# Taking one DMA engine's share of two stores away: a batched A·Bᵀ kernel, where part of two stores moves to GpSimd's DMA queue

## Chip, cores and metric

The kernel runs on one core of one Trainium2 chip. The metric is device time in microseconds (us) of one execution, the median of several runs. Before the change it is 125.15 us (three runs, 124.94 to 125.19).

## What is computed

Sixteen independent products of 512×512 float32 matrices, the second one transposed:

```python
def setup_inputs():
    batch, m, k, n = 16, 512, 512, 512
    return {"a": np.random.randn(batch, m, k).astype(np.float32),
            "b": np.random.randn(batch, n, k).astype(np.float32)}

def reference(a, b):
    return np.matmul(a, b.transpose(0, 2, 1)).astype(np.float32)
```

The inputs are 2 × 16 MiB and the output is 16 MiB, so 50.3 MB have to cross between HBM and SBUF in any case.

## The kernel before

The batches are worked in eight pairs. A load brings `a` or `b` of a whole pair (2 MiB, 16 KiB to each of 128 partitions) into one of seven slots of `ld`. VectorE casts it to bf16, TensorE transposes it into PSUM (`tp`), ScalarE and VectorE bring the transposes back (`ta`, `tb`), TensorE multiplies into `ps`, and ScalarE copies the products into one of seven slots of `ob`. SyncE stores each batch from there (1 MiB, 8 KiB from each partition).

Loads are issued by ScalarE (the trace calls this queue q10), stores by SyncE (q1), and GpSimd has a third queue (q0). All three feed the same 16 DMA engines.

```python
NL = 7; NO = 7
X = 11
ld = sbuf("ld", [P, NL, 2 * J, K], f32)
ob = sbuf("ob", [P, NO, J, N], f32)            # J = 4 rows of 512 per partition and batch
turn = sbuf("turn", [P, 4, 2, 16], f32)        # a small load's target, read by nobody
...
def load(n, engine):
    u, slot = n // 2, n % NL
    src = (a if n % 2 == 0 else b)[2 * u:2 * u + 2].rearrange("e (p j) k -> (e p) j k", j=2 * J)
    engine.dma_start(ld[:, slot], src).then_inc(s_ld[slot], 16)

def landed(n):
    return s_st[n % NO], 16 * (n // NO + 1)

def store(n, lo=0, hi=J, step=1, part=slice(0, P), engine=nc.sync):
    rows = slice(lo, hi, step)
    return engine.dma_start(
        out[n].rearrange("(p j) n -> p j n", j=J)[part, rows], ob[part, n % NO, rows])
...
# GpSimd: tells VectorE which load has landed; then its part of batch 11's store
for n in range(2 * pairs):
    nc.gpsimd.wait_ge(s_ld[n % NL], 16 * (n // NL + 1)).then_inc(s_go, 1)
nc.gpsimd.wait_ge(s_out, X + 1)
for i in range(4):
    nc.gpsimd.dma_start(turn[:5, i], a[0, :5, :64]...[:, :, :16]).then_inc(s_y, 16)
    for part in (slice(20 + i, 32, 4), slice(96 + i, P, 4)):
        store(X, step=J - 1, part=part, engine=nc.gpsimd).then_inc(s_y, 16)

# SyncE: no store before load 7 has landed
nc.sync.wait_ge(s_ld[0], 32)
for n in range(batch):
    nc.sync.wait_ge(s_out, n + 1)
    if n != X:
        store(n, hi=J if n < batch - 1 else J - 1).then_inc(landed(n)[0], 16)
        continue
    store(n, lo=1, hi=J - 1).then_inc(landed(n)[0], 16)
    store(n, step=J - 1, part=slice(32, 96)).then_inc(s_x, 16)
    for i in range(4):
        store(n, step=J - 1, part=slice(i, 16, 4)).then_inc(s_x, 16)
    store(n, step=J - 1, part=slice(16, 20)).then_inc(s_x, 16)
...
# ScalarE, per pair: its loads, then the products into ob
for e in range(2):
    n = 2 * u + e
    if n >= NO:
        nc.scalar.wait_ge(*landed(n - NO))     # the slot's earlier store has landed
    for j in range(J):
        ...                                     # copy ps -> ob[:, n % NO, j]
...
# end
nc.scalar.wait_ge(s_x, 16 * 6)
nc.scalar.wait_ge(s_y, 16 * 12)
for n in range(batch - NO, batch):
    nc.scalar.wait_ge(*landed(n))
```

[...] The four `turn` loads of five rows move nothing that is needed[...]. The other pieces of batch 11's rows 0 and 3 are cut so that engine 4[...] has less to move than the others.

Of the kernel before, what the change touches and what calls it, by code (L numbers as in the profile page):

```python
# [10 lines left out]
def kernel(  # L11
# [6 lines left out]
    nc = tc.nc  # L18
    P = 128
    batch, M, K = a.shape  # L20
    _, N, _ = b.shape
    J = M // P
# [4 lines left out]
    f32 = mybir.dt.float32  # L27
    bf16 = mybir.dt.bfloat16
    NL = 7
    NO = 7  # L30
    X = 11

    def sbuf(name, shape, dtype):
        return ctx.enter_context(nc.sbuf_tensor(name, shape, dtype))

    def sem(name):
        return tc.alloc_semaphore(name)

    with tc.tile_critical(no_gpsimd_drain=True):  # L41
# [6 lines left out]
        ta = sbuf("ta", [P, KO, 2 * J * P], bf16)  # L48
        tb = sbuf("tb", [P, KO, 2 * J * P], bf16)
        ob = sbuf("ob", [P, NO, J, N], f32)  # L50
        turn = sbuf("turn", [P, 4, 2, 16], f32)
        tp = ctx.enter_context(nc.psum_tensor("tp", [P, 4, 2 * J, P], bf16))
        ps = ctx.enter_context(nc.psum_tensor("ps", [P, 4, N], f32))

# [2 lines left out]
        s_st = [sem(f"s_st{i}") for i in range(NO)]  # L57
# [13 lines left out]
        s_out = sem("s_out")  # L71
        s_x = sem("s_x")
        s_y = sem("s_y")
# [5 lines left out]
            out=ident[:], in_=ident[:], compare_op=mybir.AluOpType.not_equal, fill=1.0,  # L79
# [6 lines left out]
        def load(n, engine):  # L86
            u, slot = n // 2, n % NL
            src = (a if n % 2 == 0 else b)[2 * u:2 * u + 2].rearrange(
                "e (p j) k -> (e p) j k", j=2 * J
            )  # L90
            engine.dma_start(ld[:, slot], src).then_inc(s_ld[slot], 16)

        def landed(n):
            return s_st[n % NO], 16 * (n // NO + 1)

        def store(n, lo=0, hi=J, step=1, part=slice(0, P), engine=nc.sync):
            rows = slice(lo, hi, step)
            return engine.dma_start(  # L98
                out[n].rearrange("(p j) n -> p j n", j=J)[part, rows], ob[part, n % NO, rows]
            )  # L100

        load(0, nc.scalar)
# [3 lines left out]

        for n in range(2 * pairs):
            nc.gpsimd.wait_ge(s_ld[n % NL], 16 * (n // NL + 1)).then_inc(s_go, 1)  # L108

        nc.gpsimd.wait_ge(s_out, X + 1)
        for i in range(4):
            nc.gpsimd.dma_start(  # L114
                turn[:5, i], a[0, :5, :64].rearrange("p (x k) -> p x k", x=2)[:, :, :16]
            ).then_inc(s_y, 16)
            for part in (slice(20 + i, 32, 4), slice(96 + i, P, 4)):
                store(X, step=J - 1, part=part, engine=nc.gpsimd).then_inc(s_y, 16)

        nc.sync.wait_ge(s_ld[0], 32)  # L120
        for n in range(batch):
            nc.sync.wait_ge(s_out, n + 1)
            if n != X:
                store(n, hi=J if n < batch - 1 else J - 1).then_inc(landed(n)[0], 16)
                continue


            store(n, lo=1, hi=J - 1).then_inc(landed(n)[0], 16)
            store(n, step=J - 1, part=slice(32, 96)).then_inc(s_x, 16)
            for i in range(4):  # L130
                store(n, step=J - 1, part=slice(i, 16, 4)).then_inc(s_x, 16)
            store(n, step=J - 1, part=slice(16, 20)).then_inc(s_x, 16)

        def taker(engine):
            return lambda s, n: engine.wait_ge(s, n).then_inc(s, -n)  # L135
# [9 lines left out]
        with nc.Fori(0, pairs, engines=[dve]) as u:  # L145
            for x, (h, w, s_c, s_w) in enumerate(
# [4 lines left out]
                if x == 0:  # L151
# [4 lines left out]
                    out=h[:, J:, :], in_=src[:, J:, :HK]  # L156
                ).then_inc(s_c, 1)
                nc.vector.tensor_copy(out=w[:], in_=src[:, :, HK:]).then_inc(s_w, 1)  # L158
            for ko in range(KO):
# [5 lines left out]
                if ko == 1:  # L165
# [3 lines left out]
                    out=tb[:, ko, :],  # L169
# [7 lines left out]
        for u in range(pairs):  # L177
            for ko in range(KO):
                nc.scalar.wait_ge(s_ta, KO * u + ko + 1)
                for e in range(2):  # L180
                    c = nc.scalar.copy(  # L181
                        out=ta[:, ko, e * J * P:(e + 1) * J * P].rearrange(
                            "k (j p h) -> k j p h", j=J, h=2
                        ),
                        in_=tp[:, ko % 2, :, e * HP:(e + 1) * HP].rearrange(
                            "k (h j) p -> k j p h", h=2
                        ),
                    )
                c.then_inc(s_ea, 1)


            for n in (2 * u + NL, 2 * u + NL + 1):
                if n < 2 * pairs:
                    load(n, nc.scalar)
            for e in range(2):
                n = 2 * u + e
                if n >= NO:
                    nc.scalar.wait_ge(*landed(n - NO))
                for j in range(J):
                    nc.scalar.wait_ge(s_mm, J * n + j + 1)  # L200
                    c = nc.scalar.copy(  # L201
                        out=ob[:, n % NO, j, :].rearrange("m (p j) -> m p j", j=2 * J),
                        in_=ps[:, j, :].rearrange("m (j p) -> m p j", j=2 * J),
                    )
                    if e == 0:
                        c.then_inc(s_pv, 1)
                    elif j in (0, J - 1):
                        c.then_inc(s_out, 1)
# [45 lines left out]


    with tc.tile_critical(sync_engine=act, no_gpsimd_drain=True):
        nc.scalar.wait_ge(s_x, 16 * 6)
        nc.scalar.wait_ge(s_y, 16 * 12)
        for n in range(batch - NO, batch):
            nc.scalar.wait_ge(*landed(n))  # L260
    waits = nc.cur_bb.bb.instructions[-1]
# [38 lines left out]
```

## Time and profile before

| what | value |
|---|---|
| time, median of 3 | 125.15 us |
| span of the profiled execution | 123.3 us |
| moved by DMA | 50.35 MB, mean 408 GB/s |
| DMA time by queue (share of 16 engines) | loads q10 60.5%, stores q1 36.2%, GpSimd q0 0.5% |
| busy share of TensorE, VectorE, ScalarE, GpSimd | 73%, 55%, 55%, 7% |
| first store issued | 42.72 us |
| last load landed | 99.78 us |
| last product copied into `ob` | 113.5 us |
| last store landed | 122.19 us |

How to read it: the profile's page gives busy times of the compute engines, then the span cut into 40 slices with the busy share of the 16 DMA engines in tenths and the GB/s they moved. A list of issues tells how long each transfer took from issue to landing. Beneath the page the trace keeps every DMA packet (queue, bytes, start and duration) and every increment of a semaphore; a transfer over all 16 engines shows 16 increments, one as each engine finishes its share, so their spread tells how far the slowest engine is behind, though not which engine it is.

### The profile page before, as it was taken

What the parts mean: (1) busy time and instruction counts of PE and PEld (TensorE: products, weight loads), DVE (VectorE), ACT (ScalarE), POOL (GpSimd) and SP (SyncE); (2) the same over time, 40 slices, a digit from 0 to 9 for tenths busy, and PEclk for the clock granted to TensorE, in tenths of its full rate; (3) what the DMA queues carried; (4) which work ended last, traced back from release to release, by engine and by line L of the source; (5) the groups of instructions that cost most, each with busy time, mean ns of one, the idle gap of its engine ahead of it and who ended that gap; (6) DMA issues with size and microseconds to landing.
All of it is one profiled execution on the core that took longest, in us unless ns stands there. A gap on an engine that the chain in (4) does not pass through costs nothing. (4 is left out here: it accounts for less than half of the span.)

```text
span 123.3 us, 2255 instructions
## 1 busy us (share of the span) xinstructions
PE 90.2 (73%) x768; PEld 54.8 (44%) x768; DVE 67.9 (55%) x96; ACT 67.9 (55%) x130; POOL 8.5 (7%) x18
## 2 busy tenths in 40 slices
PE   0000089999999899989998999999799917996000
PEld 0000078447744764574477347645654506542000
DVE  0000598982896589388918974872977059400000
ACT  0400064567855966696589468765866069656000
POOL 2000000000000000000000000000000039910000
PEclk9999999999999999999999999999999999999965
DMA  4999999999999999999999999999999999999991
GB/s 112 404 425 425 441 431 431 431 431 441 425 436 425 425 361 415 444 423 425 431 433 425 431 423 425 436 444 428 423 423 441 412 423 423 432 397 432 425 407 72
DMA packets 5341, 50.35 MB, mean 408 GB/s; under 512 B 904, under 2 KB 904, under 8 KB 1500
## 3 DMA queue, kind: packets, MB, share of 16 engines
q10 hardware_dynamic: 2160, 31.46, 60.5%
q1 hardware_dynamic: 2796, 18.70, 36.2%
q0 software_dynamic: 384, 0.18, 0.5%
q14 instruction: 1, 0.01, 0.0%
HBM read 33.56 MB, written 16.78 MB: 408 GB/s over the span
## 5 line engine op out<-in xcount | busy, mean ns | idle before, releaser
L242 PE MATMUL ps<-tb,ta 128*128 128x512 bf16 x256 | 57.8, 379 | 0.4
L201 ACT COPY ob<-ps 128x512 f32<-128x512 f32 x64 | 34.2, 591 | 27.8 <-PE ps L242 21.9
L181 ACT COPY ta<-tp 128x512 bf16<-128x512 bf16 x64 | 33.0, 612 | 13.7 <-PE tp L223 13.2
L242 PEld LDWEIGHTS ps<-tb,ta 128*128 128x128 bf16 x256 | 24.1, 98 | 30.6 <-issue 4.0
L223 PE MATMUL tp<-ident,ha 128*128 128x128 bf16 x256 | 18.6, 224 | 18.7 <-PEq L135 18.2
L223 PEld LDWEIGHTS tp<-ident,ha 128*128 128x128 bf16 x256 | 15.8, 100 | 22.3 <-issue 20.5
L168 DVE COPY tb<-tp 128x1024 bf16<-128x1024 bf16 x32 | 21.2, 685 | 3.6 <-DVEq L135 3.6
L223 PE MATMUL tp<-ident,hb 128*128 128x128 bf16 x256 | 17.6, 223 | 3.5 <-PEq L135 3.3
L223 PEld LDWEIGHTS tp<-ident,hb 128*128 128x128 bf16 x256 | 15.4, 100 | 4.7 <-issue 4.4
L154 DVE CAST ha<-ld 128x1024 bf16 x8 | 5.5, 690 | 14.6 <-POOLq L108 13.8
L163 DVE COPY ha<-wa 128x2048 bf16<-128x2048 bf16 x8 | 5.5, 691 | 12.7 <-DVEq L135 12.7
L154 DVE CAST hb<-ld 128x1024 bf16 x8 | 5.5, 689 | 7.9 <-DVEq L135 7.9
L158 DVE CAST wa<-ld 128x2048 bf16 x8 | 9.8, 1220 | 0.0
L158 DVE CAST wb<-ld 128x2048 bf16 x8 | 9.8, 1220 | 0.0
L114 POOL DMA_DIRECT2D turn<-in_a_dram x4 | 2.7, 663 | 98.9 <-ACT ob L201 98.9
L155 DVE CAST ha<-ld 128x1024 bf16 x8 | 5.5, 687 | 0.0
L155 DVE CAST hb<-ld 128x1024 bf16 x8 | 5.5, 686 | 0.0
L167 DVE COPY hb<-wb 128x2048 bf16<-128x2048 bf16 x8 | 5.5, 684 | 0.0
L98 POOL DMA_DIRECT2D out_dram<-ob x8 | 5.2, 651 | 0.0
L176 ACT ACT_TABLE_LOAD x1 | 1.3, 1283 | 4.1 <-issue 4.1
L78 POOL TENSOR_SCALAR_AFFINE_SELECT ident<-ident 128x128 bf16<-128x128 bf16 x1 | 0.3, 288 | 0.2 <-POOL ident L76 0.2
L76 POOL MEMSET ident<- 128x128 bf16 x1 | 0.2, 205 | 0.5 <-SPq L41 0.5
(5 smaller groups left out, 0.6 us busy)
## 6 DMA issues: line engine op xcount, KB each, us to landing
ld<-in_a_dram ACTq DMA_DIRECT2D x8, 2048.0 KB, 29.1
ld<-in_b_dram ACTq DMA_DIRECT2D x7, 2048.0 KB, 26.8
out_dram<-ob SPq DMA_DIRECT2D x14, 1024.0 KB, 29.0
ld<-in_b_dram SPq DMA_DIRECT2D x1, 2048.0 KB, 12.5
out_dram<-ob SPq DMA_DIRECT2D x1, 768.0 KB, 8.0
out_dram<-ob SPq DMA_DIRECT2D x1, 512.0 KB, 24.5
out_dram<-ob SPq DMA_DIRECT2D x2, 256.0 KB, 7.9
out_dram<-ob POOLq DMA_DIRECT2D x4, 32.0 KB, 6.0
```

The source lines that it names most:

```text
L98: return engine.dma_start(out[n].rearrange("(p j) n -> p j n", j=J)[part, rows], ob[part, n % NO, rows])
L114: nc.gpsimd.dma_start(turn[:5, i], a[0, :5, :64].rearrange("p (x k) -> p x k", x=2)[:, :, :16]).then_inc(s_y, 16)
L154: nc.vector.tensor_copy(out=h[:, :J, :], in_=src[:, :J, :HK])
L155: nc.vector.tensor_copy(out=h[:, J:, :], in_=src[:, J:, :HK]).then_inc(s_c, 1)
L158: nc.vector.tensor_copy(out=w[:], in_=src[:, :, HK:]).then_inc(s_w, 1)
L163: nc.vector.tensor_copy(out=ha[:], in_=wa[:]).then_inc(s_ca, 1)
L167: nc.vector.tensor_copy(out=hb[:], in_=wb[:]).then_inc(s_cb, 1)
L168: nc.vector.tensor_copy(out=tb[:, ko, :], in_=tp[:, 2 + ko % 2].rearrange("k j p -> k (j p)"),).then_inc(s_eb, 1)
L181: c = nc.scalar.copy(out=ta[:, ko, e * J * P:(e + 1) * J * P].rearrange("k (j p h) -> k j p h", j=J, h=2), in_=tp[:, ko % 2, :, e * HP:(e ...
L201: c = nc.scalar.copy(out=ob[:, n % NO, j, :].rearrange("m (p j) -> m p j", j=2 * J), in_=ps[:, j, :].rearrange("m (j p) -> m p j", j=2 * J),)
L223: t = nc.tensor.transpose(tp[:, 2 * x + g, j, :], h[:, j, g * P:(g + 1) * P], ident[:])
L242: t = nc.tensor.matmul(ps[:, j, :], ta[:, ko, (e * J + j) * P:(e * J + j + 1) * P], tb[:, ko, :].rearrange("k (j p) -> k j p", j=2 * J)[:, ...
```

## The change

Batch 11 is stored by one transfer like every other. The uneven store is moved to batches 1 and 2, whose slots lie side by side in `ob`, and is twice as large for engine 4: SyncE stores partitions 0 to 31 and 64 to 127 of both batches in two transfers; GpSimd stores partitions 32 to 61 of both in one transfer of 30 partitions, which is meant for fifteen engines, two partitions ("a pair of rows") each, with the `turn` load ahead of it placed so that engine 4 is the one left out; partitions 62 and 63 go in four small pieces after a second `turn` load. GpSimd does this right after it has passed on load 7. The waits for these transfers move from the end of the kernel to ScalarE's first reuse of their slots, at batch 8. The purpose is to take more work from the DMA engine that finishes last, and to do without the nineteen transfers (seven by SyncE, twelve by GpSimd) that batch 11 is stored with before.

```diff
-    X = 11
+    X = 1
...
-        turn = sbuf("turn", [P, 4, 2, 16], f32)
+        turn = sbuf("turn", [5, 2, 2, 16], f32)
...
         def landed(n):
-            return s_st[n % NO], 16 * (n // NO + 1)
+            return s_st[n % NO], 16 * (n // NO + (n % NO not in (X, X + 1)))
...
+        def store_two(engine, lo, hi, rows=slice(0, J)):
+            return engine.dma_start(
+                out[X:X + 2].rearrange("e (p j) n -> p e j n", j=J)[lo:hi, :, rows],
+                ob[lo:hi, X % NO:X % NO + 2, rows],
             )
...
         for n in range(2 * pairs):
             nc.gpsimd.wait_ge(s_ld[n % NL], 16 * (n // NL + 1)).then_inc(s_go, 1)
-        nc.gpsimd.wait_ge(s_out, X + 1)
-        for i in range(4):
-            ... turn load, two stores of 3 and 8 partitions ...
+            if n == NL:
+                nc.gpsimd.wait_ge(s_out, X + 2)
+                for i, parts in enumerate(((32, 62), (62, 63, 64))):
+                    nc.gpsimd.dma_start(turn[:, i], a[0, :5, :64]...[:, :, :16]).then_inc(s_y, 16)
+                    for lo, hi in zip(parts, parts[1:]):
+                        for j in range(i + 1):
+                            store_two(nc.gpsimd, lo, hi, slice(j, J, i + 1)).then_inc(s_y, 16)
...
             nc.sync.wait_ge(s_out, n + 1)
-            if n != X:
+            if n == X + 1:
+                for lo, hi in ((0, 32), (64, P)):
+                    store_two(nc.sync, lo, hi).then_inc(s_x, 16)
+            elif n != X:
                 store(n, hi=J if n < batch - 1 else J - 1).then_inc(landed(n)[0], 16)
-                continue
-            ... seven transfers of batch 11 ...
...
                 n = 2 * u + e
-                if n >= NO:
+                if n == X + NO:
+                    nc.scalar.wait_ge(s_x, 16 * 2)
+                    nc.scalar.wait_ge(s_y, 16 * 7)
+                elif n >= NO and n != X + 1 + NO:
                     nc.scalar.wait_ge(*landed(n - NO))
...
-        nc.scalar.wait_ge(s_x, 16 * 6)
-        nc.scalar.wait_ge(s_y, 16 * 12)
```

More of the change, by code (lines that the diff above doesn't have):

```diff
@@ L93, in landed, with store @@
         def landed(n):
-            return s_st[n % NO], 16 * (n // NO + 1)
-        def store(n, lo=0, hi=J, step=1, part=slice(0, P), engine=nc.sync):
-            rows = slice(lo, hi, step)
+            return s_st[n % NO], 16 * (n // NO + (n % NO not in (X, X + 1)))
+        def store(n, lo=0, hi=J):
+            return nc.sync.dma_start(
+                out[n].rearrange("(p j) n -> p j n", j=J)[:, lo:hi], ob[:, n % NO, lo:hi]
+            )
+        def store_two(engine, lo, hi, rows=slice(0, J)):
             return engine.dma_start(
-                out[n].rearrange("(p j) n -> p j n", j=J)[part, rows], ob[part, n % NO, rows]
+                out[X:X + 2].rearrange("e (p j) n -> p e j n", j=J)[lo:hi, :, rows],
+                ob[lo:hi, X % NO:X % NO + 2, rows],
             )
@@ L108 @@
             nc.gpsimd.wait_ge(s_ld[n % NL], 16 * (n // NL + 1)).then_inc(s_go, 1)
-        nc.gpsimd.wait_ge(s_out, X + 1)
-        for i in range(4):
[L114 to L118, printed above, removed]
+            if n == NL:
+                nc.gpsimd.wait_ge(s_out, X + 2)
+                for i, parts in enumerate(((32, 62), (62, 63, 64))):
+                    nc.gpsimd.dma_start(
+                        turn[:, i], a[0, :5, :64].rearrange("p (x k) -> p x k", x=2)[:, :, :16]
+                    ).then_inc(s_y, 16)
+                    for lo, hi in zip(parts, parts[1:]):
+                        for j in range(i + 1):
+                            store_two(
+                                nc.gpsimd, lo, hi, slice(j, J, i + 1)
+                            ).then_inc(s_y, 16)
         nc.sync.wait_ge(s_ld[0], 32)
@@ L122 @@
             nc.sync.wait_ge(s_out, n + 1)
-            if n != X:
+            if n == X + 1:
+                for lo, hi in ((0, 32), (64, P)):
+                    store_two(nc.sync, lo, hi).then_inc(s_x, 16)
+            elif n != X:
                 store(n, hi=J if n < batch - 1 else J - 1).then_inc(landed(n)[0], 16)
-                continue
[L128 to L132, printed above, removed]
         def taker(engine):
```

## Prediction, made before the changed kernel was run

> **What bounds the kernel now.** I read the page from its second part on, because the first already says that no compute engine is near full: TensorE is busy 73% of the span, VectorE and ScalarE 55%.
>
> ```profile
> DMA  4999999999999999999999999999999999999991
> GB/s 112 404 425 425 441 431 431 431 431 441 425 436 425 425 361 415 444 423 425 431 433 425 431 423 425 436 444 428 423 423 441 412 423 423 432 397 432 425 407 72
> ...
> q10 hardware_dynamic: 2160, 31.46, 60.5%
> q1 hardware_dynamic: 2796, 18.70, 36.2%
> q0 software_dynamic: 384, 0.18, 0.5%
> ...
> PE 6%; ACT 1%; issue 0%
> ```
>
> The DMA row has a 9 in 38 of 40 slices: the 16 engines work from start to end, at 425 to 441 GB/s in most slices. The chain of waits (last line) covers 7% of the span, so no chain of compute explains the end. Compute does wait, but for DMA:
>
> ```profile
> ACT ob L201 <- DMA out_dram<-ob: 5.9, 2, 4.4
> ...
> SPq L295 <- ACTq L256: 7.1, 1, 7.1
> ```
>
> ScalarE waits twice for an output slot whose store is late, and in the last 7.1 us SyncE waits only for landings. The timeline says how much work lies in the queues then:
>
> ```profile
> 110.77 1.07 ACT L201 COPY ob<-ps 128x512 f32<-128x512 f32 x2 [0.71 <-PE ps L242]
> 111.38 3.78 SPq L98 DMA_DIRECT2D out_dram<-ob  x3
> 112.44 1.07 ACT L201 COPY ob<-ps 128x512 f32<-128x512 f32 x2 [0.60 <-PE ps L242]
> ```
>
> The last product is ready at 113.5 us; the last store is issued at 114.33 and lands at 122.19. In between the engines work off a queue of stores. So **the end is the moment at which the last DMA engine has moved its bytes**. [...] a change of bytes on the last engine counts one for one.
>
> Which engine is last, and by how much? Each store increments its semaphore once for each of 16 engines. Batch 10's store: fifteen increments from 108.49 to 109.22 us, the sixteenth at 110.35. One engine is 1.13 us behind the next. The lag grows from store to store (0.03 us at batch 0, 0.44 at batch 3, 0.87 at batch 6). In the packet records about one in sixteen of the 8 KiB store packets between 99 and 114 us takes 320 to 360 ns, all others 309. After batch 11, which takes 16 KiB from engine 4, the last increment comes 0.5 to 0.7 us after the next (batch 15's last row: 121.61, then 122.19). That a smaller share of engine 4 halved the lag tells me that the laggard is engine 4, though the records don't name engines.
>
> [...] an engine takes turns between its queues by packets. The trace agrees: from 80 to 90 us, 176 packets of 8 KiB by q1 and 176 of 16 KiB by q10. [...]
>
> **The change, part by part.** Durations are medians of the packet records: 8 KiB 309 ns, 4 KiB 159, 2 KiB 84.
>
> Batch 11 before: each engine reads 8 × 4 KiB (rows 1 and 2) and 8 × 2 KiB (its four of the 64 partitions), 1.27 + 0.67 = 1.94 us. That is all engine 4 has. [...] After: 8 × 309 ns = 2.47 us for every engine. So engine 4 +0.53[...].
>
> Batches 1 and 2 before: 16 × 309 ns = 4.94 us on each engine. After: SyncE's 32 partitions give each engine two, its 64 give each four, at 2 × 8 KiB each: 12 packets, 3.71 us. [...] Engine 4 has none: -1.24. [...]
>
> Sum: **engine 4 -0.71 us; the others between -0.31 and +0.05.** Engine 4's last landing moves from 122.19 to 121.48. The next one, at 121.61 before, comes to 121.66 at most if it is one of those with a small piece. The end of DMA is then 121.5 to 121.7 us: **0.5 to 0.7 us gained**, nearly all that the spread allows, since the other engines can't be moved by this.
>
> What it does beside: GpSimd's seven issues (0.56 to 1.14 us each before, so about 5 us) lie between its signals for load 7 and load 8. Load 7 lands at 42.70, load 8 at 48.57, and VectorE takes load 8 only at 57.03: hidden. During some 5 us q0 takes turns with the two others, which delays the loads behind it by up to 1.2 us; the last load lands at 99.78 and the last product would be ready near 114.7 instead of 113.5, still with stores queued. The end of the kernel loses two waits that had long been met. None of this counts.
>
> **Rivals.** (1) [...] A store packet is 309 of every 920 ns of an engine's turn, so at random phase two meet in two of three turns, for 155 ns on average: about 0.1 us more a packet, and for sixteen packets 1.7 us on average, up to 3 for an unlucky pair[...]. For it: in batch 11's last small transfer, [...] one 2 KiB packet takes 241 ns and two 94 and 99. Against it: that is 0.2 us in eight packets, and reads are only a third of the traffic at that stage. It would make the time 125.2 to 127.5. (2) *Engine 4 isn't left out.* [...] Then engine 4 keeps its 1.24 and gains 0.53: 125.7. Against it: batch 11's pieces by the same queue did halve the lag. (3) *A new wait at batch 8.* ScalarE needs both stores landed at 69.19 us, when pair 4's first product is copied. Before, batch 0's store lands at 55.08 and each further MiB takes 7.3 us; 1.5 MiB more is 66.0, and 1.2 for q0 makes 67.3. It holds by 2 us without rival 1; with it ScalarE waits about 1 us, which the slack behind (1.5 us at 84.9, 4.4 at 99.8) takes up. (4) *The lag doesn't come from bytes* but from what shares the engine's path while compute runs; then it grows as before and the gain is still that of the bytes taken. This changes nothing.
>
> **Range and chances.** Without rivals 1 and 2: 125.15 - 0.55 = 124.6 us, and I give that about 55%. Rival 1 at any size that shows, 35%: 125 to 127.5. Rival 2, 10%: 125.7. The middle of this is 124.8 us; 124.2 to 126.6 should hold it 8 times in 10. A gain of 2% would need 2.5 us, more than the spread of the engines holds: 0.01. A loss of 2% (over 127.65) needs rival 1 at its worst: 0.08. Within 2%: 0.91.
>
> **What would show it.** Right: in the stores up to batch 10 the sixteenth increment comes no later than some 0.3 us after the fifteenth; q0 packets of 8 KiB between about 47 and 55 us, 60 in number; last landing 121.5 to 121.7. Rival 1: 8 KiB packets of q1 and q0 between 47 and 68 us clearly over 309 ns, fewer than 425 GB/s in those slices, and a last landing that is later although the lag of one engine is gone. Rival 2: a lag of one engine at batch 10 as large as before. Rival 3: a ScalarE wait for `s_x` or `s_y` at 69 us. I would be wrong if the queues ran empty anywhere but at the end, which a 7 or 8 in the DMA row would show.

## The result: 124.59 us, 0.4% faster

| | before | after |
|---|---|---|
| time, median of 6 runs each | 125.01 us (124.84 to 125.19) | 124.59 us (124.48 to 124.72) |
| ratio after / before, 95% interval | | 0.9966 (0.9953 to 0.9978) |
| span of the profiled execution | 123.3 us | 122.8 us |
| last two increments of batch 15's last row | 121.61, 122.19 us | 121.63, 121.64 us |
| mean of its sixteen increments | 121.39 us | 121.37 us |
| batch 10's store: last two of sixteen | 109.22, 110.35 us | 109.19, 109.20 us |

The gain is 0.42 us; the interval excludes a ratio of 1, and the gain is far within 2%. The last three rows carry the explanation. The mean over the engines has hardly moved (0.02 us); only the last one has come up to its neighbours, by 0.55 us.

The profile's slices and queue list of the kernel after, to be held against those of the prediction:

```profile
DMA  4999999999999999999999999999999999999993
GB/s 117 400 432 438 438 427 438 432 427 427 432 427 432 427 368 390 419 438 430 406 422 451 416 435 438 432 422 427 435 427 432 435 408 424 427 424 427 427 419 125
...
q10 hardware_dynamic: 2160, 31.46, 60.9%
q1 hardware_dynamic: 2528, 18.35, 35.5%
q0 software_dynamic: 272, 0.53, 1.1%
```

The queues are full throughout, as before: a 9 in 38 of 40 slices of the DMA row. 0.35 MB have moved from q1 to q0. The 397 GB/s of slice 36 (108 to 111 us), where part of batch 11's pieces were stored, is now 424.

GpSimd's timeline (start, duration, what) shows its seven issues close behind load 7:

```profile
43.38 0.69 POOL L121 DMA_DIRECT2D turn<-in_a_dram  x1 [41.69 <-DMA ld<-in_b_dram]
44.06 0.60 POOL L103 DMA_DIRECT2D out_dram<-ob  x1
44.66 0.56 POOL L121 DMA_DIRECT2D turn<-in_a_dram  x1
45.22 3.35 POOL L103 DMA_DIRECT2D out_dram<-ob  x4
```

They end at 48.6 us; VectorE wants load 8 at 57. ScalarE's wait list has changed too: the only kind that its copies into `ob` still have is for TensorE; the 5.9 us for late stores are gone.

```profile
ACT ob L209 <- PE ps L250: 25.2, 32, 1.9
```

Those 5.9 us were no part of the gain, since ScalarE isn't on the path that sets the end. The timeline of after has the last product 1.4 us later than before, and SyncE's wait list has the time in which only landings are waited for, 7.1 us before:

```profile
113.88 1.07 ACT L209 COPY ob<-ps 128x512 f32<-128x512 f32 x2 [0.60 <-PE ps L250]
```

```profile
SPq L301 <- ACTq L264: 5.3, 1, 5.3
```

The compute ends 1.4 us later, and the kernel ends earlier: both before and after, the engines work off queued stores after the last product, for 8.7 us before (113.5 to 122.19) and 6.7 after (114.95 to 121.64).

### The profile page after: what moved, and what is told of

Same layout as the page of the kernel before. It is cut to its first block, busy times and chain, and to the rows that moved or that the text cites. A ratio compares the mean times of both kernels' runs of the same rounds, so it can differ in the third digit from the quotient of the medians.

```text
span 122.8 us, 2243 instructions
## 1 busy us (share of the span) xinstructions
PE 91.2 (74%) x768; PEld 56.1 (46%) x768; DVE 68.0 (55%) x96; ACT 68.0 (55%) x130; POOL 5.9 (5%) x13
## 2 busy tenths in 40 slices
DMA packets 4961, 50.34 MB, mean 410 GB/s; under 512 B 732, under 2 KB 732, under 8 KB 996
## 5 line engine op out<-in xcount | busy, mean ns | idle before, releaser
L231 PE MATMUL tp<-ident,ha 128*128 128x128 bf16 x256 | 19.3, 230 | 18.8 <-PEq L140 18.4
L231 PEld LDWEIGHTS tp<-ident,ha 128*128 128x128 bf16 x256 | 16.5, 103 | 22.3 <-issue 20.7
L231 PE MATMUL tp<-ident,hb 128*128 128x128 bf16 x256 | 18.2, 228 | 3.8 <-PEq L140 3.5
L231 PEld LDWEIGHTS tp<-ident,hb 128*128 128x128 bf16 x256 | 16.0, 102 | 4.9 <-issue 4.6
L103 POOL DMA_DIRECT2D out_dram<-ob x5 | 4.0, 793 | 0.0
L121 POOL DMA_DIRECT2D turn<-in_a_dram x2 | 1.3, 626 | 41.7 <-DMA ld<-in_b_dram 41.7
```

Of the source, the lines that this page charges most:

```text
L103: return engine.dma_start(out[X:X + 2].rearrange("e (p j) n -> p e j n", j=J)[lo:hi, :, rows], ob[lo:hi, X % NO:X % NO + 2, rows],)
L121: nc.gpsimd.dma_start(turn[:, i], a[0, :5, :64].rearrange("p (x k) -> p x k", x=2)[:, :, :16]).then_inc(s_y, 16)
L231: t = nc.tensor.transpose(tp[:, 2 * x + g, j, :], h[:, j, g * P:(g + 1) * P], ident[:])
```

## The experiments

Two theories of the gain stood against each other. **A:** the time follows the bytes of the one engine that is last; the uneven store takes 32 KiB from it. **B:** the gain is that batch 11's nineteen transfers became one. Beside them stood the prediction's first rival: engines that meet hold each other up, which the author feared for stores over a part of the partitions. The records number no engine; "engine 4" and "engine 9" are the author's names for two of them. Times are medians; each run was timed next to the kernel before on the same chip, and the ratio to that is given, since the runs are spread over several chips. "Last" means the last two of the sixteen increments of batch 15's last row in the profiled execution.

| run | time us | ratio to before (95%) | last two increments |
|---|---|---|---|
| after, first | 124.59 | 0.9953 to 0.9978 | 121.63, 121.64 |
| after, again | 124.64 | 0.9940 to 0.9977 | 121.49, 121.50 |
| e1: engine 9 left out instead of 4 | 125.66 | 1.0031 to 1.0066 | 121.54, 122.73 |
| e2: no uneven store | 125.19 | 0.9999 to 1.0024 | 121.29, 122.40 |
| e11: quarter by q0, but even | 125.46 | 1.0023 to 1.0053 | 121.89, 122.62 |
| e5: half the relief | 124.86 | 0.9971 to 0.9996 | 121.70, 121.72 |
| e3: relieved at 1, 2 and at 11 | 125.05 | 0.9985 to 1.0012 | 121.82, 121.87 |
| e6: GpSimd's part 6 us later | 124.71 | 0.9944 to 0.9974 | 121.64, 121.70 |
| e7: batches 3 and 4 instead | 124.72 | 0.9951 to 0.9978 | 121.59, 121.71 |
| e10: small pieces meant for other engines | 124.66 | 0.9938 to 0.9977 | 121.80, 121.86 |
| e4: halves, no loads running | 126.72 | 1.0104 to 1.0170 | 122.97, 123.15 |
| e8: the same, grouped | 129.65 | 1.0306 to 1.0396 | 126.44, 126.98 |
| e9: grouped halves, loads running | 124.46 | 0.9924 to 0.9968 | 121.56, 121.58 |

### Leave out another engine

```diff
-turn = sbuf("turn", [5, 2, 2, 16], f32)
+turn = sbuf("turn", [10, 2, 2, 16], f32)
 # first turn load: a[0, :10, :64] instead of a[0, :5, :64]; the second turn load is dropped
```

> The changed kernel with one thing different: the first turn load has ten rows instead of five, so that GpSimd's transfer of 30 partitions should leave out engine 9 and give engine 4 its two partitions [...]. Theory A (the gain is the 32 KiB taken from engine 4): engine 4 is late again by 4 packets of 309 ns, the last store lands near 122.7 us, one increment about 1 us behind the next, time about 125.6. Theory B (the gain is that batch 11's nineteen transfers became one): nothing changes, 124.6.

Measured: 125.66 us, 1.07 more than after; the last landing is at 122.73 where 122.7 was expected. The last increment is again alone, 1.19 us behind the next. And now one engine is ahead: the first increment comes at 120.07, the second at 120.97. The DMA row and the last slices of this run:

```profile
DMA  4999999999999999999999999999999999999990
GB/s 111 418 434 429 423 434 434 434 444 434 423 423 423 429 341 413 407 441 431 409 434 439 429 421 434 434 434 429 426 415 447 429 407 426 426 426 434 425 386 22
```

The last two slices fell from 419 and 125 GB/s to 386 and 22: most engines are done while one still works (the span, and so the slice, is 1% longer here). Five rows more in a load that nobody reads decide a full microsecond. In the packet records the last engine has four 8 KiB packets of GpSimd's queue here, and none in after (see the laggard, below). Theory A holds, and theory B, which had 124.6 for this run, falls as the whole of the explanation.

### No uneven store

```diff
-if n == X + 1: ... store_two(nc.sync, ...)          # and GpSimd's part
-elif n != X: store(...)
+store(...)                                          # every batch alike, SyncE alone
```

> No uneven store at all: every batch, 1, 2 and 11 too, is one transfer of SyncE's queue, and GpSimd issues none. Theory A: engine 4 has all its bytes, last landing near 122.7 us with a lag of about 1.1, time 125.6 to 125.8, slower than the kernel before as well. Theory B: 124.5 to 124.6, since batch 11 is one transfer here too.

Measured: 125.19 us in 22 runs (124.86 to 125.77), so 0.6 us slower than after and 0.1 slower than before, which the interval doesn't tell from nothing. The last increment stands 1.11 us behind the next. The direction is A's, and B's 124.5 is out; the size is not A's: 125.6 to 125.8 was expected. By the way the transfers are cut, engine 4 has the same bytes here as in e1, and yet the time is 0.47 less. The next run is about that.

### The quarter by GpSimd's queue, but even

```diff
-for i, parts in enumerate(((32, 62), (62, 63, 64))): ...   # turn loads, 30 partitions, small pieces
+store_two(nc.gpsimd, 32, 64).then_inc(s_y, 16)             # 32 partitions, all 16 engines
```

> The changed kernel with GpSimd's part made even: partitions 32 to 63 of batches 1 and 2 in one transfer, two partitions for each of 16 engines, engine 4 among them, and no turn loads or small pieces. Every engine then has exactly the bytes of the run without an uneven store (125.19), but the quarter still goes by GpSimd's queue. With engine 9 left out and engine 4 loaded as fully, the time was 125.66. If the 0.47 us between those two is the price of the way by GpSimd's queue, this run is at 125.5 to 125.7; if it is not (chance, or what leaving engine 9 out gives to the others), at 125.2. Theory A in both cases: one increment about 1.1 us behind the next at the end.

Measured: 125.46 us, at the lower edge of what a price of the way would give. Its ratio to before (1.0023 to 1.0053) lies all but clear above that of e2 (0.9999 to 1.0024), with the transfers cut so that each engine has the same bytes. So **storing the two batches in this way costs about 0.3 us**. But e11 differs from e2 in three things at once: a quarter goes by GpSimd's queue, SyncE stores the rest as 32 and 64 partitions, and batch 1 is not stored until batch 2 is ready. Which of them costs is not shown. The last increment is 0.73 us behind the next, not the 1.1 expected; here the next is itself 0.37 us behind the third.

The packet records suggest a place for the price: between 42 and 52 us, when stores begin, 16 KiB load packets take longer than their 611 ns. Summed and divided by 16 engines that is 0.47 us in e2 and 0.48 before, 0.80 in e11, 0.77 in e1, 0.68 in after. A second trace of after has 0.58, though, and e10, which is as fast as after, 0.82, so this does not settle it.

The gain of the change is thus a difference. From e11 to after, which store in nearly the same way, the relief of engine 4 is worth 0.9 us by the ratios (1.0038 and 0.9966), and from e1 to after 1.07 us by the times. Less some 0.3 us for the way, that leaves the 0.6 us between e2 and after, of which the kernel before may already have had 0.1.

### Half the relief

```diff
-for i, parts in enumerate(((32, 62), (62, 63, 64))):
+for i, parts in enumerate(((32, 47), (47, 48))):
-for lo, hi in ((0, 32), (64, P)):
+for lo, hi in ((0, 32), (48, P)):
```

> The changed kernel with half the relief: GpSimd stores partitions 32 to 46 of batches 1 and 2 (fifteen partitions, one for each of fifteen engines, none for engine 4) and partition 47 in two small pieces; SyncE stores 0 to 31 and 48 to 127. Engine 4 has 16 KiB less than in a full store instead of 32. Theory A (time follows the bytes of the last engine): against the run with engine 9 left out, whose last landing was 122.73 us, two packets of 309 ns less, so 122.1 us with a lag of about 0.5, time 125.0 to 125.1, half way between 124.6 and 125.66. If another thing than engine 4's bytes counted: 124.6 as with the full relief.

Measured: 124.86 us (22 runs, 124.69 to 125.49), between full relief and none but nearer to full. In the profiled execution two engines are last together, at 121.70 and 121.72, the others at 121.44 or before. The second 16 KiB bring only some 0.2 us more (to 124.59 and 124.64). That fits a laggard which has already reached the next engine, so that a straight line in bytes was the wrong picture. It does not explain the first 16 KiB: from e1 to e5 they bring 0.80 us, although two packets are 0.62. Half as much goes by GpSimd's queue in e5, so the price of the way may be smaller too; no run tests that.

### Relieve it twice

```diff
+if n == 11: ... the seven pieces of before (SyncE)     # and GpSimd's twelve, after a turn load of 15 rows
```

> The changed kernel with batch 11 stored in its nineteen old pieces [...], so engine 4 is relieved twice. Theory A: engine 4 is no longer last, so taking more from it gains nothing, and the others get what it loses[...]; last landing 121.7 to 121.95, time 124.7 to 124.9. Theory B: the old pieces bring the old time back, 125.0 or more.

Measured: 125.05 us. The last landing, 121.87 us, lies in the expected 121.7 to 121.95, and no engine stands alone; the mean of the increments is 121.64, 0.3 later than in after. From the last landing to the reported time this execution took 3.12 us, others 2.84 to 3.1, which would account for most of the 0.15 us by which the time lies above A's range. It is also the time that B gave, and that of the kernel before (ratio 0.9999): with batch 11's pieces kept, the new uneven store gains nothing. That is the true part of B: once engine 4 isn't last, the pieces are more packets (5581 in all, 4961 in after) and more work for the others (the mean that is 0.3 us later), and dropping them was needed for the gain.

### Later, or on other batches

```diff
-if n == NL:
+if n == NL + 1:          # e6: GpSimd's part after load 8
```

> The changed kernel with GpSimd's part issued after load 8 instead of after load 7, 6 us later. Between 42 and 52 us the load packets take longer than their 611 ns, 0.68 us per engine in sum against 0.48 in the kernel before. Theory D (the added 0.2 us comes from GpSimd's queue starting together with the first stores): the sum falls to 0.5, time about 124.4. Theory E (it comes from SyncE's transfers of 32 and 64 partitions, or is chance): it stays at 0.6 to 0.7, time 124.6. ScalarE may wait 1 us for the small pieces at 69 us, which should cost nothing.

```diff
-X = 1
+X = 3                    # e7: batches 3 and 4, with n == NL + 1
```

> The whole uneven store moved from batches 1 and 2 to 3 and 4: SyncE's two transfers and GpSimd's part are issued near 50 us, when stores have long started. Theory D and theory E (if it is SyncE's uneven transfers at the start): the sum of late load packets between 42 and 52 us falls to 0.5 us, time about 124.4. If it is chance: 124.6.

Measured: 124.71 and 124.72 us, not told apart from after (124.59, 124.64). The late load packets between 42 and 52 us sum to 0.76 us in e6 and 0.54 in e7. Theory D gets no support from e6: moving GpSimd's start away from the first stores doesn't bring the sum down. In e7 it came down, but some packets were late between 52 and 62 us instead (0.13 us against 0.01 in after), and the time didn't follow. No gain from a later moment shows, but 0.2 us of time is near what these runs resolve, and what in the way of storing costs stays open. ScalarE's possible wait for the small pieces did not come: at 69 us e6 waits for TensorE, as after does. The runs also show that the relief works as well at either of these two later moments, with loads still running.

### Small pieces elsewhere

```diff
-turn[:, i],            a[0, :5, :64]...
+turn[:(5, 13)[i], i],  a[0, :(5, 13)[i], :64]...
```

The second `turn` load is longer here, to bring the four small pieces to other engines; the three cases of the expectation are that the last engines lose a piece, that they get one, and that nothing is seen.

> The changed kernel with the second turn load of 13 rows instead of 5[...]. Theory A says the last engine's bytes set the end: [...] the last landing is up to 0.15 us earlier and the time 124.4 to 124.5; [...] as much later, 124.7 to 124.8; it stays at 124.6 if the pieces are too small to be seen.

> The changed kernel itself again, on the chip of the two runs beside it, to have its time and its spread next to theirs: 124.6, last landing 121.6.

Measured: 124.66 us, and 124.64 for the changed kernel beside it. Nothing seen; 0.16 us an engine is under what these runs resolve. Which engines the pieces came to is not shown.

### Do halves of the partitions cost?

The expectations for e4 and e9 have two cases each: engines that read the same half hold each other up, or it costs nothing. That for e8 has one of two such engines held back by the other, or a cost as in e4. How engines would come to hold each other up was the author's assumption.

```diff
 # e4: batches 12 and 13, when no load is left: 12 low, 12 high, 13 low, 13 high
+for lo, hi in ((0, 64), (64, P)):
+    nc.sync.dma_start(out[n]...[lo:hi], ob[lo:hi, n % NO])
```

> The changed kernel with batches 12 and 13, which are stored when no load is left, each cut into two transfers of 64 partitions (0 to 63, then 64 to 127) over all 16 engines. [...] the 8 KiB packets of these two batches take about 620 ns instead of 309, 2 MiB take 9.8 us instead of 4.9, time about 129.5. [...] packets stay at 309 ns and the time at 124.6.

```diff
 # e8: 12 low, 13 low, 12 high, 13 high
+for lo, hi in ((0, 64), (64, P)):
+    for m in (12, 13):
+        nc.sync.dma_start(out[m]...[lo:hi], ob[lo:hi, m % NO])
```

> The changed kernel with batches 12 and 13 again in halves, but in the order 12 low, 13 low, 12 high, 13 high (64 partitions each) instead of 12 low, 12 high, 13 low, 13 high. The first order cost 1.5 us at the last landing, not the 4.9 expected. [...] the held-back engine waits 8 packets of 309 ns instead of 4, so the last landing is about 2.5 us behind the changed kernel's 121.64, and the first engines' is not late. If the cost was per transfer or by chance: 1.5 us again.

```diff
 # e9: as e8, with batches 4 and 5, stored while loads run
```

> The same grouped halves as in the run that cost 5 us (64 low partitions of two batches, then their 64 high ones), but of batches 4 and 5, which are stored while loads still take two thirds of each engine's time. [...] (rival 1 as the prediction has it: two engines meet in two of three turns, 0.1 us more a packet on average, 16 packets): 8 KiB packets over 309 ns between 70 and 92 us, last landing 1.5 us or more later, time 126 or more. [...] packets at 309 ns, time 124.6 to 124.7.

Measured, at the last landing against after: e4 1.5 us later (the profiled execution, at 126.08 us, is the shortest of four; the longest took 128.78), e8 5.3 us later, e9 not later. The time of e9, 124.46 us, is the lowest median of all, but its interval overlaps those of after, so no version here is shown to beat the changed kernel. The stretches of 9 us in which the halves of e4 and e8 are stored, and the same stretch of after; columns: stretch, its length, busy times of TensorE, weight loads, VectorE, ScalarE and GpSimd, clock, DMA share, GB/s. First after:

```profile
111.00:120.00 9.00, 3.28 (x16) 1.27 (x13) 0.00 (x0) 2.65 (x6) 0.00 (x0) 0.86 1.00 421
```

then e4:

```profile
111.00:120.00 9.00, 4.39 (x21) 1.77 (x19) 0.00 (x0) 3.22 (x6) 0.00 (x0) 0.91 1.00 387
```

then e8:

```profile
111.00:120.00 9.00, 4.10 (x19) 1.65 (x17) 0.00 (x0) 3.22 (x6) 0.00 (x0) 0.85 1.01 267
```

and, over the stretch in which e9 stores its halves, e9 and then after:

```profile
70.00:90.00 20.00, 17.94 (x158) 10.85 (x156) 13.07 (x19) 13.54 (x27) 0.00 (x0) 1.00 1.00 426
...
70.00:90.00 20.00, 17.56 (x150) 10.43 (x148) 12.44 (x18) 13.67 (x27) 0.00 (x0) 1.00 1.01 431
```

A DMA share of 1.01 at 267 GB/s is the form of this loss: the engines count as busy, and their packets take longer. In e8's worst slice the page has 215 GB/s:

```profile
GB/s 143 414 430 420 445 420 420 430 455 414 420 430 420 394 338 448 399 451 409 432 425 443 425 437 414 440 420 440 417 443 422 414 420 435 422 287 215 287 345 40
```

That is half of 430. The packets show it singly: between 111 and 121 us, 135 of e8's 329 packets of 8 KiB take over 500 ns (up to 1396), and 25 of e4's 366. In e9, between 70 and 92 us, one of 365 is over 340 ns. So stores over half the partitions do hold each other up where they follow each other without a load in between, to 215 GB/s at the worst; among loads, in e9 (426 GB/s), no such cost shows. What makes them do so is not shown. The staggering that the expectation for e8 had (2.5 us) is too small by half, and the first engines are late as well, by 2.9 us; e8 is close to the plain halving (16 packets of 309 ns, 4.9 us) that was first expected of e4. Why e4's order escapes most of it isn't settled.

## Why the prediction was right

**The bound** (the end is when the last DMA engine has moved its bytes): shown. In after the last product came 1.4 us later and the end 0.5 us earlier; it followed the last engine.

**The laggard is engine 4, and it counts one for one:** shown by e1, with "4" as a name for the engine that GpSimd's transfer of 30 partitions passes over in after: the step that takes 1.24 us from it in the prediction (4 packets of 309 ns) is worth 1.07 us of time, since the next engine then takes over. (e5's first 16 KiB brought more than their bytes, so "one for one" holds only roughly.)

The packet records allow a closer identification than the prediction made. Between 99 and 114 us, 37 of after's store packets of 8 KiB take over 311 ns. Together they last 12.15 us of a stretch of 14.5, and yet no two overlap by more than 13 ns: 31 of the 36 gaps between them are within 13 ns of zero, and the other five are as long as one to three normal packets. So one engine ran them one after another. Followed back from packet to packet to 49 us, the engine with the long packets has none of the sixty 8 KiB packets of GpSimd's queue in after, and four of them in e1. Laid end to start in the same way, all packets of after between 44 and 70 us form sixteen chains: fifteen have four of the sixty each (1.24 us), eight of these also one 4 KiB piece (159 ns), and one has none of either. The slow engine is thus the one that the change leaves out.

**The sum** (-0.71 for engine 4, the next one at 121.66 at most, last landing 121.5 to 121.7): 121.64 measured, and 121.50 in the second profile. The central case of 124.6 us was met; the 124.8 on record was pulled up by rivals that didn't come true. The gain in time, 0.42 us, is a little under the 0.5 to 0.7 forecast: over six runs the kernel before has 125.01, not the 125.15 that the prediction set out from. What the other engines lose or gain in it (-0.31 to +0.05) is the author's estimate, since no record names the engines. The 44 packets of 4 KiB by q0 in before come in four rounds of eleven: 4 × 159 ns = 0.64 us more for each of eleven engines, if each takes one of every round. The 40 of 2 KiB that q1 has beside the even 128 make 10 × 84 ns = 0.84 us on four. One store of 8 × 309 ns instead leaves the eleven with 0.11 us less and the four with 0.31 less, and a small piece adds 0.16.

**"None of this counts":** here the working missed a term. The new way of storing costs about 0.3 us (e2 to e11), which the sum doesn't have. It shows in the mean of the last increments: by the sum it should fall by 0.1 us, and load 0 alone landed 0.11 us earlier in the profiled execution; it fell by 0.02, so some 0.2 us are missing. The last landing was met in part by luck: that quicker start made up for about half of it.

**Rival 1 (engines that meet):** real, but not here. The estimate from phase (0.1 us a packet, 1.7 us in all, from 309 ns in 920) took two engines that meet to be served in turn, which was an assumption; it is refuted by after and e9: between 46 and 68 us one of 410 store packets in after takes over 340 ns. For batches stored after the last load it would have been right in kind, and too small in size (5.3 us in e8).

**Rival 2 (engine 4 not left out):** refuted by the chains of after and by e1, which has the time that this rival implied (125.66 us, 125.7 implied) when engine 4 does get its two partitions.

**Rival 3 (new wait at batch 8):** SyncE's second transfer landed at 67.76 us (67.3 worked out), the last small piece at 64.26, both before ScalarE begins batch 8. The timeline has it wait for TensorE there, not for a store:

```profile
69.10 1.08 ACT L209 COPY ob<-ps 128x512 f32<-128x512 f32 x2 [1.18 <-PE ps L250]
```

**Rival 4 (the lag isn't made by bytes but grows with compute):** without weight for the gain, as the prediction said. Between 99 and 114 us, 35 of before's 644 store packets of 8 KiB take over 311 ns, and 37 of after's 750. In before, too, they follow each other on one engine (with a gap of 2.1 us while it moved batch 11's smaller pieces); over the normal 309 ns they add up to 0.76 us before and 0.72 after. The engine is as slow as it was; it has only been given a start. Whether the compute engines cause this is not shown.

## What to carry to other kernels

When a kernel keeps all DMA engines busy to the end, look at the sixteen increments of its late stores: one that stands alone is time to gain, and the gain ends where the second slowest engine stands (here 0.58 us at batch 15's last row, and 0.42 us gained). Give such an engine less at a stage where the queues are full and loads run among the stores: three moments there did equally well, and splitting stores into halves of the partitions showed no cost there (e9, 124.46 us), while the same split among stores alone halved the rate at its worst (215 GB/s). Count what the uneven store itself costs, here some 0.3 us of 0.9 gained. Check the relief by leaving out another engine instead: if that brings no loss, the relief wasn't what gained.

## What the runs showed that I had not expected

The store packets of 8 KiB that run long between 99 and 114 us (312 to 361 ns instead of 309), in before and after alike, belong to one engine, the laggard; why its packets take longer stays open. Stores of half the partitions showed no cost among loads (e9) and cost up to 5.3 us among stores (e8). And an uneven way of storing two batches, a quarter of it by GpSimd's queue, cost about 0.3 us (e11 against e2) even where the transfers were cut to give every engine the same bytes.
